# The low half of k in the score matmuls: a 64-row operand becomes a 128-row operand with 64 rows of zeros

## The chip, the cores and the metric

The kernel runs on one core of a Trainium2 chip. The metric is device time in microseconds (us) of that core, lower is better. TensorE is written PE (its weight loads PEld), VectorE DVE, ScalarE ACT, GpSimd POOL, and SP is the engine whose queue issues the DMAs.

## The reference, cut to what matters

One decoder layer over 272 rows (16 meta tokens and 256 positions), model width 2048, in float32. After a norm, one projection feeds eight attention heads and four retention heads; then an output projection, a gated MLP with a short convolution, and a last norm. The change concerns the scores of the attention heads. Each head h has two maps m = 0, 1 of depth 64:

```
aq, ak, av, rq, rk, rv, rg = jnp.split(proj, SPLITS, axis=-1)
...
s = jnp.einsum('bqhmd,bkhmd->bhmqk', qb, k).astype(jnp.float32) * scale
...
p = jax.nn.softmax(s, axis=-1)
a = (p[:, :, 0] - lam * p[:, :, 1]).astype(v.dtype)
return jnp.einsum('bhqk,bkhe->bqhe', a, v)
```

## The kernel before, in words

Float32 products are made from fp32r operands. A value x is split into hi (x rounded to fp32r) and lo (x - hi), and a product is the sum hi*hi + hi*lo + lo*hi.

**The projections (`gemm`, L243).** Activations lie with the model width over the 128 partitions, as `xhi` and `xlo`. Each block of 128 output columns takes 16 steps over the width, and each step three matmuls (L262 to L264) into one PSUM tile `mm`. The weights come by DMA as chunks of 1 MB (`raw`, three buffers, L87). ACT rounds each half chunk to `whi` (L99), DVE takes `wlo` as the difference (L100), three buffers each; `ahead` keeps two half chunks prepared beyond the one in use. After every quarter of a gemm, `pump` takes tasks from the list `side`: that is how attention work gets between the projection's matmuls. The framework's scheduler then fixes one order for each engine; the engines run their own order and meet by semaphores.

**The scores (L303).** A head's q and k stand in one tile of 128 partitions, map 0 in partitions 0 to 63 and map 1 in 64 to 127. From these the kernel makes, for each map m, a tile with all 128 partitions in use: `q2[:, m]` holds hi of q in the map's own 64 partitions (`hs`) and lo of q in the other 64 (`os`); `k2[:, m]` holds hi of k in both. So one matmul over 128 rows (L310) gives hi*hi + lo*hi. The third product, hi of q with lo of k, is a second matmul (L312) over the 64 partitions `hs` only, with lo of k in a tile `kl` of 128 x 272. A score task i (0, 1, 2) covers 86 queries and the first 100, 186 or 272 keys, and issues four matmuls: L310 and L312 for map 0, then L310 and L312 for map 1. The stationary operand, which PE loads first, is q (86 columns); k streams past it. There are 8 heads x 3 tasks = 24 score tasks, 96 matmuls, 48 of them at L312.

**The residual.** `htok` (128 x 2 x 2048 float32, 16 KB of each partition) is written only from the output projection on (L552) and lies unused before.

Of the kernel before, what the change touches and what calls it, by code (L numbers as in the profile page):

```python
# [10 lines left out]
F32 = mybir.dt.float32  # L11
F32R = mybir.dt.float32r
# [7 lines left out]
P = 128  # L20
D = 2048
# [3 lines left out]
T = META + SEQ  # L25
Q0 = META - 2
NQ = T - Q0
QT = NQ // 3
# [25 lines left out]
def trunk_kernel(ctx, tc, a, out):  # L54
# [84 lines left out]
    rstd1 = cp.tile([P, T], F32, name="rstd1")  # L139
    rstd2 = cp.tile([P, NQ], F32, name="rstd2")  # L140

    htok = big.tile([P, 2, D], F32, name="htok")
    ps1 = ctx.enter_context(tc.tile_pool(name="ps1", bufs=1, space=PSUM))

    def misc(name):
# [123 lines left out]
    with ExitStack() as p1:  # L269
# [5 lines left out]
        def row_rstd(ss, width, name):  # L275
# [7 lines left out]
            V.tensor_tensor(out=r, in0=r, in1=fin, op=ALU.mult)  # L283
            return r

        nop = lambda: None

        def att_tasks(h, q, k, v):
            slope = 2.0 ** (-(h + 1))
            tasks = []  # L290
            As = {}
            vt = ap_.tile([P, 3, P], F32, tag="vt", name=f"vt{h}")
            at = [ap_.tile([P, 3 - j, QT], F32, tag=f"at{j}", name=f"at{h}_{j}")
                  for j in range(3)]
            bias = ap_.tile([QT, 3, T], F32, tag="bias", bufs=1, name=f"bias{h}")

            def prelude():
                S.activation(out=bias, in_=base, func=AF.Copy, scale=slope)

            yo = ap_.tile([QT, 3, P], F32, tag="yo", name=f"yo_{h}")  # L300
            ss = sp.tile([QT, 3], F32, tag="ss3", name=f"ss{h}")

            def scores(i):  # L303
                def f():
                    nk = KB[i][1]
                    ps = ps1.tile([P, 2, 512], F32, tag="sc", bufs=1, name=f"sc{h}_{i}")
                    for m in range(2):
                        hs = slice(m * 64, (m + 1) * 64)
                        qs = slice(i * QT, (i + 1) * QT)
                        PE.matmul(ps[:QT, m, :nk], q[:, m, qs], k[0][:, m, :nk],  # L310
                                  start=True, stop=False)
                        PE.matmul(ps[:QT, m, :nk], q[hs, m, qs], k[1][hs, :nk],  # L312
                                  start=False, stop=True)
                    t = ap_.tile([QT, 2, T], F32, tag="t", name=f"t{h}_{i}")
                    nm = sp.tile([QT, 2], F32, tag="nm", name=f"nm{h}_{i}")
                    for m in range(2):
                        V.tensor_tensor_reduce(out=t[:, m, :nk], in0=bias[:, i, :nk],
                                               in1=ps[:QT, m, :nk], scale=-1.0, scalar=3.0e38,
                                               op0=ALU.add, op1=ALU.min,
                                               accum_out=nm[:, m:m + 1])  # L320
                    e = ap_.tile([QT, 2, T], F32, tag="e", name=f"e{h}_{i}")
                    sm = sp.tile([QT, 2], F32, tag="sm", name=f"sm{h}_{i}")
                    for m in range(2):
                        S.activation(out=e[:, m, :nk], in_=t[:, m, :nk], func=AF.Exp,
                                     bias=nm[:, m:m + 1], scale=-1.0,
                                     accum_out=sm[:, m:m + 1])
                    V.reciprocal(out=sm, in_=sm)
                    V.tensor_tensor(out=sm[:, 1:2], in0=sm[:, 1:2], in1=nlam[:QT], op=ALU.mult)
                    V.tensor_scalar(out=e[:, 0, :nk], in0=e[:, 0, :nk], scalar1=sm[:, 0:1],
                                    scalar2=None, op0=ALU.mult)  # L330
                    A = ap_.tile([QT, T], F32, tag="A", bufs=3, name=f"A{h}_{i}")
                    V.scalar_tensor_tensor(out=A[:, :nk], in0=e[:, 1, :nk], scalar=sm[:, 1:2],
                                           in1=e[:, 0, :nk], op0=ALU.mult, op1=ALU.add)
                    As[i] = A
                return f

            def vtr():
                ps = misc(f"pv{h}")
                for j, (b, e) in enumerate(KB):
                    PE.transpose(ps[:e - b, j * P:(j + 1) * P], v[:, b:e], idt)  # L340
                V.tensor_copy(out=vt[:KB[0][1], 0], in_=ps[:KB[0][1], :P])
                V.tensor_copy(out=vt[:QT, 1:3].rearrange("p a b -> p (a b)"),
                              in_=ps[:QT, P:3 * P])

            def atr(i):
                def f():
                    ps = misc(f"pa{h}_{i}")
                    for j in range(i + 1):
                        b, e = KB[j]
                        PE.transpose(ps[:e - b, j * P:j * P + QT], As[i][:, b:e], idt[:QT, :QT])  # L350
                    for j in range(i + 1):
                        b, e = KB[j]
                        (V.tensor_copy if j else S.copy)(
                            out=at[j][:e - b, i - j], in_=ps[:e - b, j * P:j * P + QT])
                return f

            def av():
                ps = misc(f"po{h}")
                for i in range(3):
                    for j in range(i + 1):  # L360
                        n = KB[j][1] - KB[j][0]
                        PE.matmul(ps[:QT, i * P:(i + 1) * P], at[j][:n, i - j], vt[:n, j],  # L362
                                  start=(j == 0), stop=(j == i))
                for i in range(3):
                    S.activation(out=yo[:, i], in_=ps[:QT, i * P:(i + 1) * P], func=AF.Square,
                                 accum_out=ss[:, i:i + 1])
                r = row_rstd(ss, P, f"ms{h}")
                for i in range(3):
                    S.activation(out=yo[:, i], in_=ps[:QT, i * P:(i + 1) * P], func=AF.Copy,
                                 scale=r[:, i:i + 1])  # L370

            def ytr():
                ps = misc(f"py{h}")
                for i in range(3):
                    PE.transpose(ps[:, i * QT:(i + 1) * QT], yo[:, i], idt[:QT, :QT])
                S.activation(out=yhi[:, h], in_=ps[:, :NQ], func=AF.Copy, scale=sub8)
                V.scalar_tensor_tensor(out=ylo[:, h], in0=ps[:, :NQ], scalar=sub8,
                                       in1=yhi[:, h].bitcast(F32), op0=ALU.mult,
                                       op1=ALU.subtract)

            return [prelude, scores(0), scores(1), vtr, scores(2), atr(0), atr(1), atr(2),
                    nop, av, nop, ytr]
# [94 lines left out]
        for h in range(AH):  # L477
            q = ap_.tile([P, NQ], F32, tag="q", name=f"q{h}")
            k = ap_.tile([P, T], F32, tag="k", name=f"k{h}")
            v = ap_.tile([P, T], F32, tag="v", name=f"v{h}")  # L480
            ps = gemm(idx, xhi, xlo, Q0, NQ, 1)
            V.scalar_tensor_tensor(out=q, in0=ps[:, :NQ], scalar=0.125, in1=rq_,
                                   op0=ALU.mult, op1=ALU.mult)
            ps = gemm(idx + 1, xhi, xlo, 0, T, 1)
            V.tensor_tensor(out=k, in0=ps[:, :T], in1=rk_, op=ALU.mult)
            ps = gemm(idx + 2, xhi, xlo, 0, T, 1)
            V.tensor_tensor(out=v, in0=ps[:, :T], in1=rk_, op=ALU.mult)
            idx += 3
            q2 = ap_.tile([P, 2, NQ], F32R, tag="q2", name=f"q2_{h}")
            k2 = ap_.tile([P, 2, T], F32R, tag="k2", name=f"k2_{h}")  # L490
            kl = ap_.tile([P, T], F32R, tag="kl", name=f"kl_{h}")
            for m in range(2):
                hs, os = slice(m * 64, m * 64 + 64), slice(64 - m * 64, 128 - m * 64)
                S.copy(out=q2[hs, m], in_=q[hs])
                V.tensor_tensor(out=q2[os, m], in0=q[hs], in1=q2[hs, m].bitcast(F32),
                                op=ALU.subtract)
                S.copy(out=k2[hs, m], in_=k[hs])
                V.tensor_copy(out=k2[os, m], in_=k[hs])
                V.tensor_tensor(out=kl[hs], in0=k[hs], in1=k2[hs, m].bitcast(F32),
                                op=ALU.subtract)  # L500
            side.extend(att_tasks(h, q2, (k2, kl), v))
        for kind, r in RSEQ:
# [16 lines left out]
            for c in range(2):  # L519
# [8 lines left out]
        ghi = Halves([big.tile([P, HK, NQ], F32R, tag=f"acthi{i}", name=f"ghi{i}")  # L528
                      for i in range(2)])
        glo = big.tile([P, KT, NQ], F32R, tag="actlo", name="glo")  # L530
        acc2 = yp.tile([P, NQ], F32, name="acc2")
        for j in range(KT):
            xr = ap_.tile([P, NQ], F32, tag="g0", name=f"xres{j}")
# [215 lines left out]
```

## Time and profile before

| | |
|---|---|
| time of three runs | 1216.55 to 1217.88 us, median 1217.49 us |
| span of the profiled execution | 1215.7 us (1.8 us less than the median) |
| PE busy, PEld busy | 98%, 93% of the span |
| DVE, ACT, POOL busy | 65%, 46%, 0% of the span |
| chain of work that ended last | PE 95%, DMA 2%, DVE 2% |

The profiled execution's own time is its span and the launch around it, which the span leaves out. The starts of matmuls and weight loads are recorded; the ends of matmuls are modelled, so what a matmul costs PE is read from its start to the start of the next one, called its pitch below. An engine's "busy" says little about whether it is at its peak.

### The profile page before, as it was taken

How to read it: one execution, taken by the hardware profiler on the slowest of the kernel's cores; microseconds unless marked ns; L12 is line 12 of the kernel's file. 1: busy time of each engine (PE TensorE's matmuls, PEld its weight loads, DVE VectorE, ACT ScalarE, POOL GpSimd, SP SyncE). 2: the span in 40 equal slices, each digit the busy share in tenths (PEclk: the TensorE clock that was granted, in tenths of full speed). 3: DMA queues.
4: the chain of work that ended last, by engine and by line, in shares of the span. 5: the costliest groups of instructions: out<-in, count | busy, mean ns of one | idle time of the engine just before them, and what ended most of it. 6: DMA issues, size and time to landing. Idle time of an engine off the chain costs nothing.

```text
span 1215.7 us, 21284 instructions
## 1 busy us (share of the span) xinstructions
PE 1196.5 (98%) x8811; PEld 1135.3 (93%) x8811; DVE 790.7 (65%) x1423; ACT 558.3 (46%) x865; POOL 0.8 (0%) x5
## 2 busy tenths in 40 slices
PE   7999999999999999999999999999999999999996
PEld 6999999999999999999999999999999988888885
DVE  6877787667786557666666666666666645454544
ACT  6465665544445554444444444444444434343442
POOL 0000000000000000000000000000000000000000
PEclk9999999999999999999999999999999999999998
DMA  8443343444445555554554554554555654555552
GB/s 295 149 168 108 140 142 138 163 165 146 153 164 200 196 191 175 193 188 174 189 193 174 184 198 174 179 197 180 177 195 184 210 202 177 196 185 187 194 180 98
DMA packets 34817, 215.71 MB, mean 177 GB/s; under 512 B 4194, under 2 KB 7882, under 8 KB 9760
## 3 DMA queue, kind: packets, MB, share of 16 engines
q1 hardware_dynamic: 34288, 212.58, 49.8%
q8 instruction: 69, 1.13, 0.4%
q0 software_dynamic: 144, 1.05, 0.3%
q10 hardware_dynamic: 288, 0.72, 0.2%
q14 instruction: 28, 0.23, 0.1%
HBM read 212.24 MB, written 2.10 MB: 176 GB/s over the span
## 4 chain that ended last, share of the span: by engine, by line
PE 95%; DMA 2%; DVE 2%; SPq 0%; ACT 0%; issue 0%; DVEq 0%; ACTq 0%
PE mm L262 23%; PE mm L263 23%; PE mm L264 23%; PE o L608 7%; PE o L609 7%; PE o L610 7%; DMA raw<-in_w_first_dram 1%; PE sc L312 1%; PE po L362 1%; PE sc L310 1%; DMA xr<-in_x_dram 1%; DVE wlo L100 0%; PE pa L350 0%; PE rs L402 0%; PE ph L551 0%
## 5 line engine op out<-in xcount | busy, mean ns | idle before, releaser
L99 ACT CAST whi<-raw 128x1024 fp32r<-128x1024 f32 x381 | 399.7, 1049 | 566.1 <-PE mm L263 309.0
L100 DVE TENSOR_TENSOR wlo<-raw,whi 128x1024 fp32r<-128x1024 f32 x381 | 466.3, 1224 | 280.9 <-ACT whi L99 278.0
L262 PE MATMUL mm<-ghi,whi 128*128 128x258 f32 (+1 forms) x1408 | 396.9, 282 | 0.0
L264 PE MATMUL mm<-ghi,wlo 128*128 128x258 f32 (+1 forms) x1408 | 396.7, 282 | 0.0
L263 PE MATMUL mm<-glo,whi 128*128 128x258 f32 (+1 forms) x1408 | 396.1, 281 | 0.0
L263 PEld LDWEIGHTS mm<-glo,whi 128*128 128x128 f32 x1408 | 266.4, 189 | 0.0
L262 PEld LDWEIGHTS mm<-ghi,whi 128*128 128x128 f32 x1408 | 266.0, 189 | 0.0
L264 PEld LDWEIGHTS mm<-ghi,wlo 128*128 128x128 f32 x1408 | 265.8, 189 | 0.0
L262 PE MATMUL mm<-xhi,whi 128*128 128x272 f32 (+1 forms) x688 | 201.5, 293 | 0.0
L263 PE MATMUL mm<-xlo,whi 128*128 128x272 f32 (+1 forms) x688 | 199.3, 290 | 0.0
L264 PE MATMUL mm<-xhi,wlo 128*128 128x272 f32 (+1 forms) x688 | 197.9, 288 | 0.6 <-DVE wlo L100 0.6
L609 PE MATMUL o<-wlo,fhi 128*128 128x512 f32 x340 | 134.1, 395 | 0.0
L610 PE MATMUL o<-whi,flo 128*128 128x512 f32 x340 | 134.1, 395 | 0.0
L262 PEld LDWEIGHTS mm<-xhi,whi 128*128 128x128 f32 x688 | 129.6, 188 | 1.5
L264 PEld LDWEIGHTS mm<-xhi,wlo 128*128 128x128 f32 x688 | 129.5, 188 | 1.0 <-DVE wlo L100 0.8
L263 PEld LDWEIGHTS mm<-xlo,whi 128*128 128x128 f32 x688 | 129.6, 188 | 0.7
L608 PE MATMUL o<-whi,fhi 128*128 128x512 f32 x340 | 120.8, 395 | 0.0
L609 PEld LDWEIGHTS o<-wlo,fhi 128*128 128x128 f32 x340 | 64.0, 188 | 15.0
L610 PEld LDWEIGHTS o<-whi,flo 128*128 128x128 f32 x340 | 64.1, 188 | 14.9
L608 PEld LDWEIGHTS o<-whi,fhi 128*128 128x128 f32 x340 | 64.0, 188 | 14.9
L262 PE MATMUL mm<-yhi,whi 128*128 128x258 f32 x256 | 73.3, 288 | 0.4 <-ACT whi L99 0.4
L263 PE MATMUL mm<-ylo,whi 128*128 128x258 f32 x256 | 72.4, 284 | 0.0
(226 smaller groups left out, 1071.4 us busy)
## 6 DMA issues: line engine op xcount, KB each, us to landing
raw<-in_w_in_dram SPq DMA_DIRECT2D x44, 1024.0 KB, 4.9
raw<-in_w_gate_dram SPq DMA_DIRECT2D x44, 1024.0 KB, 4.8
raw<-in_w_up_dram SPq DMA_DIRECT2D x44, 1024.0 KB, 4.8
raw<-in_w_down_dram SPq DMA_DIRECT2D x44, 1024.0 KB, 4.8
raw<-in_w_out_dram SPq DMA_DIRECT2D x16, 1024.0 KB, 4.9
xres<-in_x_dram SPq DMA_DIRECT2D x16, 129.0 KB, 3.8
raw<-in_w_first_dram SPq DMA_DIRECT2D x2, 1024.0 KB, 13.9
raw<-in_w_first_dram SPq DMA_DIRECT2D x3, 512.0 KB, 7.3
```

The lines of the kernel that those rows point to most:

```text
L99: S.copy(out=hi, in_=src)
L100: V.tensor_tensor(out=lo, in0=src, in1=hi.bitcast(F32), op=ALU.subtract)
L262: PE.matmul(ps[:, :n], wh, xh, start=(k == 0), stop=False)
L263: PE.matmul(ps[:, :n], wh, xl, start=False, stop=False)
L264: PE.matmul(ps[:, :n], wl, xh, start=False, stop=(k == KT - 1))
L310: PE.matmul(ps[:QT, m, :nk], q[:, m, qs], k[0][:, m, :nk], start=True, stop=False)
L312: PE.matmul(ps[:QT, m, :nk], q[hs, m, qs], k[1][hs, :nk], start=False, stop=True)
L362: PE.matmul(ps[:QT, i * P:(i + 1) * P], at[j][:n, i - j], vt[:n, j], start=(j == 0), stop=(j == i))
L608: PE.matmul(po[m], ah, wh, start=(k == 0), stop=False)
L609: PE.matmul(po[m], ah, wl, start=False, stop=False)
L610: PE.matmul(po[m], al, wh, start=False, stop=(k == NF - 1))
```

## The change

`kl` of each head moves out of the attention pool into a tile `klz` of 128 partitions x 2 slots (even and odd heads) x 2 maps x 272. `klz` takes the room of `htok`, which is now allocated after the attention and retention stage. Once, at the program's start, POOL sets to zero the 64 partitions of each map that hold no k (two instructions of 64 x 2 x 272). DVE writes lo of k into the map's own partitions as before, 64 x 272 for each map. The matmul at L312 (L315 afterwards) then takes all 128 partitions of `q2[:, m]` as stationary operand and all 128 of `klz` as the moving one: lo of q meets the zeros.

```
-    htok = big.tile([P, 2, D], F32, name="htok")
...
+        klz = big.tile([P, 2, 2, T], F32R, tag="htok", name="klz")
+        for m in range(2):
+            os = slice(64 - m * 64, 128 - m * 64)
+            nc.gpsimd.memset(klz[os, :, m].bitcast(F32), 0.0)
...
-                        hs = slice(m * 64, (m + 1) * 64)
                         qs = slice(i * QT, (i + 1) * QT)
                         PE.matmul(ps[:QT, m, :nk], q[:, m, qs], k[0][:, m, :nk],
                                   start=True, stop=False)
-                        PE.matmul(ps[:QT, m, :nk], q[hs, m, qs], k[1][hs, :nk],
+                        PE.matmul(ps[:QT, m, :nk], q[:, m, qs], k[1][:, m, :nk],
                                   start=False, stop=True)
...
-            kl = ap_.tile([P, T], F32R, tag="kl", name=f"kl_{h}")
+            kl = klz[:, h % 2]
...
-                V.tensor_tensor(out=kl[hs], in0=k[hs], in1=k2[hs, m].bitcast(F32),
+                V.tensor_tensor(out=kl[hs, m], in0=k[hs], in1=k2[hs, m].bitcast(F32),
                                 op=ALU.subtract)
...
+        htok = big.tile([P, 2, D], F32, tag="htok", name="htok")
```

The lines of the changed kernel are shifted: L262 to L264 become L261 to L263, L310 and L312 become L313 and L315. Apart from lines and buffer names, the rows of PE, DVE, ACT and SP stand in the same order as before, row for row. On POOL two rows are new. Before, at the program's start and end:

```order
L730 MEMSET const-float32-1.0 128x1
L730 MEMSET const-bfloat16-1.0 128x1
L730 MEMSET const-uint8-127 128x1
L738 UNCONDITIONAL_BRANCH [waits barrier_Pool_Activation_PE_DVE_SP_gather]
L592 DMA fn<-in_final_norm_dram 128x2048 [waits DVE_49,PE_49]
```

And in the changed kernel, with the memsets of `klz` ahead of the one DMA of that queue:

```order
L734 MEMSET const-float32-1.0 128x1
L734 MEMSET const-bfloat16-1.0 128x1
L734 MEMSET const-uint8-127 128x1
L742 UNCONDITIONAL_BRANCH [waits barrier_Pool_Activation_PE_DVE_SP_gather]
L288 MEMSET klz 64x2x272 x2
L596 DMA fn<-in_final_norm_dram 128x2048 [waits DVE_49,PE_49]
```

They wait for nothing of the kernel's own. On PE the first score task stands between two matmuls of the k projection. Before:

```order
L264 MATMUL mm_797<-xhi_68,wlo_736 128x272
L310 MATMUL sc_0_534<-k_0_462,q_0_461 86x100 [waits DVE_49]
L312 MATMUL sc_0_534<-kl_463,q_0_461 86x100
L310 MATMUL sc_0_534<-k_0_462,q_0_461 86x100
L312 MATMUL sc_0_534<-kl_463,q_0_461 86x100
L262 MATMUL mm_797<-xhi_68,whi_735 128x272
```

And in the changed kernel:

```order
L263 MATMUL mm_797<-xhi_68,wlo_736 128x272
L313 MATMUL sc_0_535<-k_0_464,q_0_463 86x100 [waits DVE_49]
L315 MATMUL sc_0_535<-klz,q_0_463 86x100 [waits Pool_49]
L313 MATMUL sc_0_535<-k_0_464,q_0_463 86x100
L315 MATMUL sc_0_535<-klz,q_0_463 86x100 [waits Pool_49]
L261 MATMUL mm_797<-xhi_68,whi_735 128x272
```

No row has moved; the two low matmuls of this first task now wait for the two memsets. Two more instructions gain that wait, both the first of their engine to write `htok`: ACT's first copy into it and DVE's first sum into it.

## Rows read from the trace of the kernel before

**Rows 1.** The page: the span, and the ending chain by engine.

```profile
span 1215.7 us, 21284 instructions
...
PE 95%; DMA 2%; DVE 2%; SPq 0%; ACT 0%; issue 0%; DVEq 0%; ACTq 0%
```

**Rows 2.** Busy time by stretch: engines, granted TensorE clock, DMA share, GB/s.

```profile
160.00:190.00 30.00, 30.00 (x232) 28.08 (x230) 24.31 (x84) 17.80 (x50) 0.00 (x0) 1.00 0.35 123
...
sum 154.00, PE 154.00 PEld 143.50 DVE 116.93 ACT 90.73 POOL 0.00; mean PE 30.80 PEld 28.70 DVE 23.39 ACT 18.15 POOL 0.00
```

**Rows 3.** Waits of PE between 58 and 290 us (total, times, longest).

```profile
PE mm L264 <- DVE wlo L100: 0.6, 1, 0.6
```

**Rows 4.** Tile `sc`: count, min/median/max ns, first and last start, forms.

```profile
L312 PE MATMUL sc<-kl,q x48: 275/314/354, 61.9 to 214.0; 64*86 64x100 f32 x16, 64*86 64x186 f32 x16, 64*86 64x272 f32 x16
```

**Rows 5.** Timeline of PE, first score task (start, length, engine, line).

```profile
61.73 0.21 PE L310 MATMUL sc<-k,q 128*86 128x100 f32 x1
...
62.08 0.28 PE L310 MATMUL sc<-k,q 128*86 128x100 f32 x1
62.29 0.28 PE L312 MATMUL sc<-kl,q 64*86 64x100 f32 x1
62.49 0.39 PE L262 MATMUL mm<-xhi,whi 128*128 128x272 f32 x1
62.73 0.28 PE L263 MATMUL mm<-xlo,whi 128*128 128x272 f32 x1
...
62.98 0.29 PE L262 MATMUL mm<-xhi,whi 128*128 128x272 f32 x1
```

**Rows 6.** Timeline of PE's weight loads in the same stretch.

```profile
61.61 0.15 PEld L310 LDWEIGHTS sc<-k,q 128*86 128x86 f32 x1
...
62.49 0.19 PEld L262 LDWEIGHTS mm<-xhi,whi 128*128 128x128 f32 x1
62.60 0.19 PEld L263 LDWEIGHTS mm<-xlo,whi 128*128 128x128 f32 x1
```

**Rows 7.** Timeline of PE, second score task of head 0.

```profile
66.63 0.25 PE L310 MATMUL sc<-k,q 128*86 128x186 f32 x1
...
67.78 0.29 PE L264 MATMUL mm<-xhi,wlo 128*128 128x272 f32 x1
```

**Rows 8.** Timeline of PE, third score task of head 0.

```profile
71.03 0.29 PE L310 MATMUL sc<-k,q 128*86 128x272 f32 x1
...
72.34 0.29 PE L263 MATMUL mm<-xlo,whi 128*128 128x272 f32 x1
```

**Rows 9.** Timeline of PE, L310 followed by matmuls over 86 rows.

```profile
133.07 0.21 PE L310 MATMUL sc<-k,q 128*86 128x100 f32 x1
133.12 0.39 PE L350 MATMUL pa<-c_ident,A 86*100 86x86 f32 x3
...
137.60 0.25 PE L310 MATMUL sc<-k,q 128*86 128x186 f32 x1
137.69 0.49 PE L362 MATMUL po<-vt,at 86*86 86x128 f32 x3
```

**Rows 10.** Weight loads by shape, 58 to 290 us (busy us, mean ns).

```profile
L262 PEld LDWEIGHTS mm<-xhi,whi 128*128 128x128 f32 x495 | 93.2, 188 | 1.4
L310 PEld LDWEIGHTS sc<-k,q 128*86 128x86 f32 x48 | 7.3, 153 | 2.3
```

**Rows 11.** Timeline of the program's start: memsets.

```profile
0.35 0.09 POOL L730 MEMSET const-uint8-127<- 128x1 uint8 x1
...
1.14 0.27 DVE L138 MEMSET warm<- 128x256 uint32 x1
```

**Rows 12.** Timeline of PE at the end of the first four projections.

```profile
30.05 0.58 PE L190 MATMUL mm<-xhi,whi 128*128 128x258 f32 x1 [3.88 <-ACT whi L182]
```

**Rows 13.** Timeline: one half chunk's `wlo` on DVE, its first matmul on PE.

```profile
76.34 1.22 DVE L100 TENSOR_TENSOR wlo<-raw,whi 128x1024 fp32r<-128x1024 f32 x1
...
80.02 0.29 PE L264 MATMUL mm<-xhi,wlo 128*128 128x272 f32 x1
```

## The prediction

> **What bounds the kernel now.** I read the page's chain first: PE holds 95% of what ended last, DMA and DVE 2% each [rows 1], so time taken from PE's sequence comes off the end unless another engine turns late. Next the stage in which the score tasks lie, 61 to 215 us: in the 154 us of the five stretches that cover it PE is busy for all 154.00, DVE for 116.93 (76%), ACT for 90.73 (59%), and the granted clock is 1.00, the 2.4 GHz level, in the stretch shown [rows 2]. Then PE's waits: between 58 and 290 us PE waited once, 0.6 us, for `wlo` [rows 3], and that is before the first score task. So PE is never held up by anything in this stage, and "busy" hides only what PE does badly by itself. That is read from starts alone.
>
> The first score task shows it. A projection matmul of 272 columns has a pitch of 0.125 us (62.73 to 62.98 is two of them). A score matmul streams only 100 columns, yet the 64-row one at 62.29 takes 0.20 us to the next start, and the projection matmul behind it takes 0.24 (62.49 to 62.73), double its usual pitch [rows 5]. The weight loads say why. For the L310 that follows a projection matmul, the load starts at 61.61, 0.12 us before its matmul starts at 61.73: loaded under the matmul ahead. The load for the projection matmul behind a 64-row matmul starts at 62.49, together with its matmul, and the next load is let go only at 62.60 [rows 5, 6]. On both sides of a 64-row matmul the load is not hidden; between 128-row matmuls it is. L310 itself has 86 columns of weights and short streams, so neither of these explains it. Nor does a row count below 128 as such: L310 of 100 columns followed by a matmul over 86 rows has a pitch of 0.05 us, and L310 of 186 columns one of 0.09 [rows 9]. What is special is 64.
>
> **The change part by part.** It removes the only 64-row matmuls, 48 of them, all between 61.9 and 214.0 us [rows 4]. I price one score task from the start of its first L310 to the start of the second projection matmul behind it, so that the doubled pitch is inside.
>
> Now: task 0 takes 62.73 - 61.73 = 1.00 us [rows 5], task 1 67.78 - 66.63 = 1.15 [rows 7], task 2 72.34 - 71.03 = 1.31 [rows 8]; together 3.46 us a head.
>
> After: five pitches each, with loads hidden. A pitch is the longer of its own stream and the next weight load. Loads: two loads of 128 columns follow each other after 0.11 us when nothing else holds them (62.49 to 62.60) [rows 6]; a load of 86 columns lasts 153 ns against 188 [rows 10], 35 ns less, so I take 0.074 us. Streams: 0.05 us for 100 columns, 0.09 for 186 [rows 9], 0.125 for 272 [rows 5].
> - Task 0: three pitches bound by an 86-column load, 3 x 0.074, one by the projection's 128-column load, 0.11, one projection matmul, 0.125: 0.457 us.
> - Task 1: 3 x 0.09 + 0.11 + 0.125 = 0.505 us.
> - Task 2: 5 x 0.125 = 0.625 us.
>
> Together 1.587 us a head, 1.87 less than now; eight heads give 15.0 us. Some tasks of later heads have transposes or value matmuls between the first L310 and its L312; these cost the same in both kernels, and the 64-row pitches around them are the same kind, so I price all heads like head 0.
>
> No row has two neighbouring 128-row loads of 86 columns, so 0.074 is an estimate from these rows. Its bounds: not below the stream of 0.05, not above the 128-column load of 0.11. With 0.05 task 0 gains 0.07 more, 0.6 us over eight heads. With 0.11 in tasks 0 and 1 the loss is 3 x 0.036 + 3 x 0.02 = 0.17 a head, 1.3 us. So PE gives back 13.7 to 15.6 us.
>
> That the matmuls stream 128 rows instead of 64 costs nothing extra: the 128-row L310 and the 64-row L312 of one task have the same pitch, 0.21 and 0.20 us from 62.08 on, where each stands beside the other [rows 5].
>
> Row against rule: the rows show that the load behind a 64-row matmul starts late, the load behind a 128-row one early [rows 5, 6]. The Trainium skill, "TensorE: Matmul & The Clock Gate", section on LDWEIGHTS, says that a weight load is priced by its columns, not by the rows it covers, 32 rows costing what 128 cost; its table of practical hints says the same of a single matmul of few rows. By that rule alone the edit would be worth 0, by the rows it is worth 15.0 us; the trace agrees with the rule on a single load (0.15 us for either row count) but not on when it may start.
>
> The zeros: two memsets of 64 x 544 on POOL, 1088 columns in all. The trace has no such POOL row. Bounds: DVE's memset of 256 columns took 0.27 us, 1.05 ns a column, so 1.1 us; POOL's memsets of one column took 0.09 us each [rows 11], which per column would be 98 us. I take the first, because 0.09 us for one column is what any small instruction costs, and price it at nothing: POOL has no other work, and the first reader is L312 at 61.9 us [rows 4], some 60 us later. Should the memsets hold up DVE or PE at the start, by a microsecond, PE's idle 3.88 us before 30.05 covers it [rows 12]; without that cover it would cost its own 1.1 us.
>
> At no cost either: DVE's writes into `klz` are the same 64 x 272, with the same waits; the slot of head h is written again for head h + 2, as with the two buffers before. The added waits on `htok` are for memsets long done. SP's rows are unmoved.
>
> **What is late next.** PE comes earlier by up to 15 us, so DVE and ACT must prepare weights faster: DVE's share of the stage rises from 76% to 116.93 / 139 = 84%, in the fullest stretch from 24.31 / 30 = 81% to about 90% [rows 2]. The preparation follows PE's releases, so it moves along; the smallest lead that I find inside the stage is the `wlo` that ends at 77.56 and is first read at 80.02, 2.46 us [rows 13]. By then four score tasks have given back 2.4 us, but DVE's own chain starts from those tasks' outputs and comes earlier too. I count no loss.
>
> Sum on the profiled execution: 1215.7 - 15.0 = 1200.7 us; the median of the runs stands 1.8 us above that span, so **1202.5 us**.
>
> **The rivals.**
> 1. The rows don't matter (the change doesn't do what it says): what holds the loads is the short 86-column operand. For: L310 has a pitch of 0.21 us inside the task too [rows 5]. Against: the projection matmul behind the task suffers too, and L310 behind a projection matmul does not. Time: 1217.5. Chance 5%.
> 2. DVE or ACT turn into the bound of the stage: half the gain is lost in waits for `wlo`. For: DVE near 90% and a lead of 2.46 us. Against: no wait in the stage now. Time: 1217.5 - 7.5 = 1210. Chance 5%.
> 3. Slower: POOL's memset is priced by the column at POOL's small rows. It would end near 0.4 + 98 us, L312 would wait from 61.9 to 98.4, 36.5 us, with every PE row behind it: 1202.5 + 36.5 = 1239. It costs from 61.5 us of memset on, and turns the sign at 61.5 + 15 + 2.4 = 79 us. For: only POOL's rows of one column are known. Against: four of those in a row were done 0.44 us into the span [rows 11]. Chance 4%.
>
> **How the numbers follow.** The forecast has 86%: 1202.5 us, with 13.7 to 15.6 us of gain and 0.7 us of spread between runs, that is 1201.2 to 1204.5. I widen it to 1200.8 to 1205.5 for a small loss in waits or a little more gain than the streams allow; this leaves out the rivals and about 5% of the forecast's own case. A difference of 0.2%, 2.4 us, is about what a measurement of this kernel can tell from no change. Faster: the forecast and rival 2, 91%. Same: rival 1, 5%. Slower: rival 3, 4%.
>
> **What would show it.** In the changed trace the loads of L315 and of the rows behind them start under the matmul ahead; pitches inside a task are near 0.075, 0.09 and 0.125 us, and no projection matmul behind a task takes 0.23. Head 0's three tasks, measured as above, sum to 1.6 us instead of 3.46. POOL shows two memsets of about a microsecond together, and PE no wait on POOL. Everything from 216 us on is the same work, 15 us earlier. The prediction is wrong if L315 still drags its load, if PE's waits in 61 to 200 us sum to more than a microsecond, or if the memsets reach 61 us.

## The result, and the profile after

The changed kernel takes 1201.6 us (median; 1200.84 to 1204.27) against 1217.4 us before: ratio 0.9878, 95% interval 0.9867 to 0.9890, which is 15.8 us less. 1202.5 us had been forecast.

The page of the changed kernel, its span, and the ending chain by engine and by line:

```profile
span 1199.9 us, 21288 instructions
...
PE 95%; DMA 2%; DVE 2%; SPq 0%; ACT 0%; issue 0%; DVEq 0%; ACTq 0%
PE mm L261 24%; PE mm L262 24%; PE mm L263 23%; PE o L612 7%; PE o L614 7%; PE o L613 7%; DMA raw<-in_w_first_dram 1%; PE po L365 1%; DMA xr<-in_x_dram 1%; PE sc L315 0%; PE sc L313 0%; DVE wlo L100 0%; PE pa L353 0%; PE rs L405 0%; SPq L165 0%
```

PE still holds 95% of the chain; in the full row, the two lines of the scores fell from 1% each to 0%. The first score task on PE's timeline, which answers to [rows 5]:

```profile
60.92 0.21 PE L313 MATMUL sc<-k,q 128*86 128x100 f32 x1
60.96 0.24 PE L315 MATMUL sc<-klz,q 128*86 128x100 f32 x1
61.04 0.24 PE L313 MATMUL sc<-k,q 128*86 128x100 f32 x1
61.12 0.24 PE L315 MATMUL sc<-klz,q 128*86 128x100 f32 x1
61.19 0.35 PE L261 MATMUL mm<-xhi,whi 128*128 128x272 f32 x1
61.38 0.29 PE L262 MATMUL mm<-xlo,whi 128*128 128x272 f32 x1
```

From the first start to the second projection matmul it takes 0.46 us instead of 1.00. The weight loads of the same stretch, which answer to [rows 6]:

```profile
60.80 0.15 PEld L313 LDWEIGHTS sc<-k,q 128*86 128x86 f32 x1
60.92 0.15 PEld L315 LDWEIGHTS sc<-klz,q 128*86 128x86 f32 x1
60.99 0.16 PEld L313 LDWEIGHTS sc<-k,q 128*86 128x86 f32 x1
61.07 0.16 PEld L315 LDWEIGHTS sc<-klz,q 128*86 128x86 f32 x1
61.15 0.19 PEld L261 LDWEIGHTS mm<-xhi,whi 128*128 128x128 f32 x1
61.26 0.19 PEld L262 LDWEIGHTS mm<-xlo,whi 128*128 128x128 f32 x1
```

Every load now starts 0.04 to 0.12 us before its matmul, also those of L315 and of the projection behind it; loads of 86 columns follow each other every 0.08 us. The other two tasks of head 0 on PE's timeline, from the first start to the second projection matmul behind as in [rows 7, 8], take 0.50 and 0.62 us instead of 1.15 and 1.31:

```profile
65.28 0.25 PE L313 MATMUL sc<-k,q 128*86 128x186 f32 x1
...
65.78 0.29 PE L263 MATMUL mm<-xhi,wlo 128*128 128x272 f32 x1
...
69.02 0.28 PE L313 MATMUL sc<-k,q 128*86 128x272 f32 x1
...
69.64 0.29 PE L262 MATMUL mm<-xlo,whi 128*128 128x272 f32 x1
```

The stage is now 139 us long. Its busy sums (PE, PEld, DVE, ACT, POOL) from the view by stretches, and PE's only wait between 40 and 275 us, which lies before the first score task (at 57 us) as it did in [rows 3]:

```profile
sum 139.00, PE 139.00 PEld 139.00 DVE 115.39 ACT 90.17 POOL 0.00; mean PE 27.80 PEld 27.80 DVE 23.08 ACT 18.03 POOL 0.00
```

```profile
PE mm L263 <- DVE wlo L100: 0.5, 1, 0.5
```

DVE's share is 115.39 / 139 = 83%. The lead that was smallest before [rows 13] is still the smallest of the stage; it has shrunk but holds; the `wlo` on DVE ends at 75.23 and is first read at 76.79, 1.56 us later:

```profile
74.00 1.23 DVE L100 TENSOR_TENSOR wlo<-raw,whi 128x1024 fp32r<-128x1024 f32 x1
...
76.79 0.29 PE L263 MATMUL mm<-xhi,wlo 128*128 128x272 f32 x1
```

**A measure that leaves out the start.** The way to the first score task differs by some microseconds between profiled executions (last section). So for each kernel I also give the time from the start of its first score matmul to the start of its last matmul, read from its one profiled execution. How far it can be trusted shows in kernels that should agree: the changed kernel, e4, e6 and e7 lie within 0.1 us of each other, the kernel before and e1 within 0.2 us.

| kernel | us, median | ratio, 95% interval | first score to last matmul, us | gain on it |
|---|---|---|---|---|
| before | 1217.4 | | 1143.8 | |
| after | 1201.6 | 0.9867 to 0.9890 | 1128.8 | 15.0 |
| e1, layout alone | 1217.2 | 0.9984 to 1.0003 | 1143.7 | 0.1 |
| e2, map 1 alone | 1208.5 | 0.9912 to 0.9941 | 1136.1 | 7.7 |
| e3, 64 rows, side by side | 1207.5 | 0.9905 to 0.9935 | 1134.4 | 9.4 |
| e4, map 0 over 96 rows | 1200.7 | 0.9847 to 0.9876 | 1128.9 | 14.9 |
| e5, without low product | 1199.4 | 0.9842 to 0.9871 | 1125.5 | 18.3 |
| e6, long memsets | 1202.4 | 0.9868 to 0.9897 | 1128.8 | 15.0 |
| e7, 128 rows in e3's order | 1201.9 | 0.9860 to 0.9893 | 1128.9 | 14.9 |
| e8, 64 rows, cut in two | 1209.4 | 0.9918 to 0.9955 | 1136.3 | 7.5 |

### The profile page after: what moved, and what is told of

It is laid out like the page before. It is cut to its first block, busy times and chain, and to the rows that moved or that the text cites. A ratio compares the mean times of both kernels' runs of the same rounds, so it can differ in the third digit from the quotient of the medians.

```text
span 1199.9 us, 21288 instructions
## 1 busy us (share of the span) xinstructions
PE 1183.2 (99%) x8811; PEld 1132.3 (94%) x8811; DVE 790.1 (66%) x1423; ACT 557.5 (46%) x865; POOL 2.0 (0%) x7
## 4 chain that ended last, share of the span: by engine, by line
PE 95%; DMA 2%; DVE 2%; SPq 0%; ACT 0%; issue 0%; DVEq 0%; ACTq 0%
PE mm L261 24%; PE mm L262 24%; PE mm L263 23%; PE o L612 7%; PE o L614 7%; PE o L613 7%; DMA raw<-in_w_first_dram 1%; PE po L365 1%; DMA xr<-in_x_dram 1%; PE sc L315 0%; PE sc L313 0%; DVE wlo L100 0%; PE pa L353 0%; PE rs L405 0%; SPq L165 0%
## 5 line engine op out<-in xcount | busy, mean ns | idle before, releaser
L261 PE MATMUL mm<-ghi,whi 128*128 128x258 f32 (+1 forms) x1408 | 396.9, 282 | 0.0
L263 PE MATMUL mm<-ghi,wlo 128*128 128x258 f32 (+1 forms) x1408 | 396.7, 282 | 0.0
L262 PE MATMUL mm<-glo,whi 128*128 128x258 f32 (+1 forms) x1408 | 396.1, 281 | 0.0
L262 PEld LDWEIGHTS mm<-glo,whi 128*128 128x128 f32 x1408 | 266.4, 189 | 0.0
L261 PEld LDWEIGHTS mm<-ghi,whi 128*128 128x128 f32 x1408 | 266.0, 189 | 0.0
L263 PEld LDWEIGHTS mm<-ghi,wlo 128*128 128x128 f32 x1408 | 265.8, 189 | 0.0
L261 PE MATMUL mm<-xhi,whi 128*128 128x272 f32 (+1 forms) x688 | 200.4, 291 | 0.0
L262 PE MATMUL mm<-xlo,whi 128*128 128x272 f32 (+1 forms) x688 | 198.8, 289 | 0.0
L263 PE MATMUL mm<-xhi,wlo 128*128 128x272 f32 (+1 forms) x688 | 197.8, 288 | 0.5 <-DVE wlo L100 0.5
L263 PEld LDWEIGHTS mm<-xhi,wlo 128*128 128x128 f32 x688 | 129.5, 188 | 0.8 <-DVE wlo L100 0.8
L261 PEld LDWEIGHTS mm<-xhi,whi 128*128 128x128 f32 x688 | 129.7, 188 | 0.1
L262 PEld LDWEIGHTS mm<-xlo,whi 128*128 128x128 f32 x688 | 129.6, 188 | 0.1
L613 PEld LDWEIGHTS o<-wlo,fhi 128*128 128x128 f32 x340 | 64.1, 188 | 14.9
L612 PEld LDWEIGHTS o<-whi,fhi 128*128 128x128 f32 x340 | 64.0, 188 | 14.9
L261 PE MATMUL mm<-yhi,whi 128*128 128x258 f32 x256 | 73.2, 288 | 0.4 <-ACT whi L99 0.4
L262 PE MATMUL mm<-ylo,whi 128*128 128x258 f32 x256 | 72.3, 283 | 0.0
```

The costliest lines, as they stand in the source:

```text
L261: PE.matmul(ps[:, :n], wh, xh, start=(k == 0), stop=False)
L262: PE.matmul(ps[:, :n], wh, xl, start=False, stop=False)
L263: PE.matmul(ps[:, :n], wl, xh, start=False, stop=(k == KT - 1))
L612: PE.matmul(po[m], ah, wh, start=(k == 0), stop=False)
L613: PE.matmul(po[m], ah, wl, start=False, stop=False)
```

## The experiments

**e1: the layout without the matmul.** Edit to the changed kernel:

```
+                        hs = slice(m * 64, (m + 1) * 64)
...
-                        PE.matmul(ps[:QT, m, :nk], q[:, m, qs], k[1][:, m, :nk],
+                        PE.matmul(ps[:QT, m, :nk], q[hs, m, qs], k[1][hs, m, :nk],
```

> The changed kernel with everything but its matmul: klz in the room of htok, the two memsets and the later htok stay, the low matmuls take 64 rows again. Theory (the whole gain comes from PE no longer changing between 128-row and 64-row matmuls): the time of before, 1217.4 us, with the three score tasks of head 0 at 1.00, 1.15 and 1.31 us. Rival (part of the gain comes from the new places in SBUF or from the later htok): between 1202 and 1216 us. If the 0.8 us that the changed kernel was ahead before its first score task came from the memsets, this run is ahead by them too, 1216.6.

1217.2 us: no gain. The three tasks of head 0 take 0.99, 1.15 and 1.30 us, as before. The rival of the layout falls. The 0.8 us by which the changed kernel's profile was ahead at its first score task (60.92 against 61.73) did not come back with the memsets: e1 has them and started its scores at 62.48. One start can't exclude a part of the memsets in it, because the starts differ by more than that (last section), and the interval of this run's time is too wide to tell 0.8 us.

**e2: only map 1 over 128 rows.** With `hs = slice(0, 64 + m * 64)` in the same matmul, map 0 keeps 64 rows.

> The changed kernel with only map 1's low matmul over 128 rows, map 0's over 64. Theory: every 64-row matmul exposes the load into it and the loads behind it, whatever else stands in the task. Worked out from pitches of before and after, the tasks take 0.73, 0.82 and 0.95 us (2.50 a head, against 3.46 and 1.59), so 7.6 us of the 15 come: 1209.8 us. Rival (one 64-row matmul spoils the whole task): under 3 us of gain, 1215 or more. Rival (what costs is map 1's matmul, whose operands start at partition 64): nearly the whole gain, 1203 or less.

1208.5 us, 7.7 us on the measure without the start, where 7.6 had been worked out, and tasks of 0.73, 0.82 and 0.95 us as expected: a 64-row matmul that stands between 128-row ones pays for itself, whatever the other map does. Both rivals fall, the one of 1215 us or more and the one of 1203 or less. PE's timeline of the first task shows both kinds:

```profile
60.08 0.21 PE L314 MATMUL sc<-k,q 128*86 128x100 f32 x1
60.22 0.28 PE L316 MATMUL sc<-klz,q 64*86 64x100 f32 x1
60.42 0.28 PE L314 MATMUL sc<-k,q 128*86 128x100 f32 x1
60.54 0.24 PE L316 MATMUL sc<-klz,q 128*86 128x100 f32 x1
60.62 0.35 PE L261 MATMUL mm<-xhi,whi 128*128 128x272 f32 x1
60.81 0.29 PE L262 MATMUL mm<-xlo,whi 128*128 128x272 f32 x1
```

Pitches of 0.14, 0.20 and 0.12 us around the 64-row matmul (into it, out of it, and the one behind), 0.08 from the 128-row low matmul to the projection.

**e3: 64 rows, both low matmuls next to each other.** Edit to the kernel before:

```
+                    qs = slice(i * QT, (i + 1) * QT)
+                    for m in range(2):
+                        PE.matmul(ps[:QT, m, :nk], q[:, m, qs], k[0][:, m, :nk],
+                                  start=True, stop=False)
                     for m in range(2):
                         hs = slice(m * 64, (m + 1) * 64)
-                        qs = slice(i * QT, (i + 1) * QT)
-                        PE.matmul(ps[:QT, m, :nk], q[:, m, qs], k[0][:, m, :nk],
-                                  start=True, stop=False)
                         PE.matmul(ps[:QT, m, :nk], q[hs, m, qs], k[1][hs, :nk],
                                   start=False, stop=True)
```

> The kernel before with one edit: in each score task both L310 first, then both 64-row low matmuls, so that PE changes once into 64 rows and once out of it. Theory (the change between row counts costs, not the 64-row matmul): the second 64-row matmul's load is hidden, tasks near 0.70, 0.84 and 0.98 us, gain 7.5 us: 1209.9 us. Rival (each 64-row matmul pays for itself): only the pitch between the two L310 shrinks, gain 3.6 us: 1213.8 us. Variant of the theory (two 64-row matmuls on different rows run side by side): a pitch near 0 between the two, gain up to 9 us, 1208.5 us. The scheduler places some other rows differently here.

1207.5 us, and tasks of 0.66, 0.76 and 0.86 us, shorter than the theory's 0.70, 0.84 and 0.98: the rival of 1213.8 falls, and the variant fits best. PE's timeline of the first task ("x2" is two matmuls in a row):

```profile
60.75 0.29 PE L309 MATMUL sc<-k,q 128*86 128x100 f32 x2
60.97 0.28 PE L313 MATMUL sc<-kl,q 64*86 64x100 f32 x2
61.18 0.39 PE L262 MATMUL mm<-xhi,whi 128*128 128x272 f32 x1
61.41 0.29 PE L263 MATMUL mm<-xlo,whi 128*128 128x272 f32 x1
```

From the first 64-row start to the projection's are 0.21 us, as from a single one in the kernel before (0.20 in [rows 5]): the second one is free, and only the change into 64 rows and the change out of it are paid, 0.66 us for this task against 0.46 in the changed kernel. The task of 272 keys shows the same with longer streams: two 64-row matmuls take 0.28 us together in e3 (69.69 to 69.97), and a single one took 0.28 in the kernel before (71.82 to 72.10), so the two streams don't follow each other. The Trainium skill, "TensorE: Matmul & The Clock Gate", Part 3 on packing small matmuls, says that matmuls on different row groups run at the same time; the trace agrees.

**e4: map 0 over 96 rows, map 1 over 128.** With `hs = slice(0, 96 + m * 32)`.

> The changed kernel with map 0's low matmul over 96 rows (64 of k, 32 of zeros), map 1's over 128. Theory (only the 64-row case makes PE change its way of working): the same as the changed kernel, 1201.6 us, all pitches the same. Rival (any operand below 128 rows drags its loads): half of the gain is lost, 1209.8 us as with map 0 over 64 rows.

1200.7 us, and 14.9 us on the measure without the start: 96 rows are as good as 128. A row count below 128 doesn't drag as such: 64 does, 96 doesn't, and other counts were not tried in this place.

**e5: no low matmul.** The second `PE.matmul` of the score task is left out, the first one stops the sum.

> The changed kernel without the low matmuls: hi of q with lo of k is left out of the scores, so this prices what the 48 zero-padded matmuls still cost. Theory (they cost their pitches of the changed kernel's trace and nothing else): two pitches of 0.076, 0.087 and 0.124 us less in the three tasks, 0.574 us a head, 4.6 us in all: 1197.0 us against 1201.6. Rival (PE is by now ahead of DVE and ACT, so that shorter tasks turn into waits): 1199 us or more, with waits of PE for wlo or for a score tile. The scheduler places other rows differently here.

1199.4 us, 3.3 us less than the changed kernel on the measure without the start, where 4.6 were expected. Summed by tile, the pitches of the score matmuls fell by 4.7 us (9.33 to 4.67), close to the 4.6 worked out; 1.4 us came back elsewhere, in rows that the scheduler had placed differently: the projections' matmuls cost 0.9 us more, of which about 0.8 in one gap at a wait for DVE, the retention's matmuls 0.9 more, and the other small matmuls 0.5 less. The time lies in the rival's range, but the wait is not one that the rival named: PE waited for `rg`, the DVE product that empties a PSUM tile of a projection, and not for `wlo` or a score tile. From the view of PE's waits:

```profile
PE mm L261 <- DVE rg L508: 0.6, 1, 0.6
```

So the zero-padded matmuls cost 4.7 us of PE's pitches; the 64-row ones, with what they did to their neighbours, cost 15.0 us more.

**e6: long memsets.** Three more memsets over the rest of the room of `htok`, 128 x 3008 each:

```
+        for c in range(3):
+            nc.gpsimd.memset(room[:, 4 * T:].bitcast(F32), 0.0)
```

> The changed kernel with POOL also setting the rest of htok's room to zero, three memsets of 128 x 3008, before the two of klz; at 0.57 us for 544 columns that is 3.2 us each, 10.6 us in all. It prices the memsets and the cover at the start. Theory (a POOL memset holds up DVE's cast of onesr until it ends, as in the changed kernel where that cast took 0.63 us instead of 0.16; the delay is covered by PE's waits for data at the start): DVE's cast takes 3 us or more, PE's first projection matmuls come up to some us later, the time stays within 1 us of the changed kernel's 1201.6. Rival (the delay stays on the path): 1204 us or more. Rival (POOL and DVE don't meet at all): the cast takes 0.16 us.

1202.4 us, and no difference on the measure without the start. The timelines of POOL and DVE (the scheduler put one long memset ahead of the two short ones):

```profile
0.74 2.60 POOL L288 MEMSET room<- 128x3008 f32 x1 [0.29 <-POOLq L737]
3.40 1.15 POOL L291 MEMSET room<- 64x544 f32 x2
...
1.33 2.09 DVE L136 CAST onesr<-one 128x128 fp32r<-128x128 f32 x1
3.54 0.50 DVE L174 SCALAR_TENSOR_TENSOR xlo<-xr,xhi 128x272 fp32r<-128x272 f32 x1
```

The cast is held until just after the long memset ends at 3.34. It was 2.09 us and not the expected 3 or more, since only one of the long memsets ran ahead of it; the rival of 0.16 falls. The next DVE instruction is not held by the memsets that still run: it takes 0.50 us, as in the kernel before. The cover named in the prediction was hardly needed, since DVE's first instruction on input data started at 3.54 here and at 3.44 in the kernel before, where no memset ran. Whether a held cast would cost anything without it was not tried.

**e7: 128 rows in e3's order.** e3's loops in the changed kernel.

> The changed kernel with the order of the run that put both 64-row matmuls side by side: both high matmuls first, then both low ones, all over 128 rows. Theory (only the row count matters, the order of 128-row matmuls doesn't): the same as the changed kernel, 1201.6 us, the pitch between the two low matmuls 0.08 to 0.125 us, not 0.003. Rival (the order alone gave part of that run's 9.9 us): faster than 1200 us.

1201.9 us, and 1128.9 on the measure without the start against 1128.8: the order is worth nothing by itself; what e3 gained, it gained by 64-row matmuls meeting.

**e8: 64-row matmuls behind each other on the same rows.** Edit to e3:

```
-                        PE.matmul(ps[:QT, m, :nk], q[hs, m, qs], k[1][hs, :nk],
-                                  start=False, stop=True)
+                        for c in (slice(0, nk // 4 * 2), slice(nk // 4 * 2, nk)):
+                            PE.matmul(ps[:QT, m, c], q[hs, m, qs], k[1][hs, c],
+                                      start=False, stop=c.stop == nk)
```

> The run with both 64-row matmuls side by side, with each of them cut into two over half of the keys: map 0 twice, then map 1 twice, so that a 64-row matmul follows another on the same rows. It asks whether the cost lies in the change between 128 and 64 rows or in 64-row weights, which might never be loaded ahead over rows that are in use. Theory (the change): the pitch between the two halves of one map is a hidden load, about 0.075 us, and 24 tasks x 0.11 us more make 2.6 us on top of that run's 1207.5: 1210.1 us. Rival (64-row weights on the same rows are never loaded ahead): that pitch is the unhidden one of before, 0.19 to 0.22 us, and the time 8.9 us more than that run's: 1216.4 us.

1209.4 us, near the theory and far from the rival's 1216.4. PE's timeline of the first task:

```profile
61.45 0.29 PE L309 MATMUL sc<-k,q 128*86 128x100 f32 x2
61.67 0.34 PE L314 MATMUL sc<-kl,q 64*86 64x50 f32 x4
61.94 0.40 PE L262 MATMUL mm<-xhi,whi 128*128 128x272 f32 x1
```

Four 64-row matmuls take 0.27 us together where e3's two took 0.21, and a single one 0.20 before: among themselves they hide their loads. So it is the change between 64 and 128 rows that costs. The starts within the four don't follow the expected even pitch (the two halves of one map are recorded 7 ns apart, the maps 91 ns), so the recorded starts inside such a group aren't read as times of work, in e3 neither; the sums over the group are.

No version beat the changed kernel without leaving work out; e4 is the same within its interval.

## Why the prediction was right

**The mechanism.** What it read from starts alone was confirmed from three sides: the gain comes with the matmul and not with the layout (e1), half of it with one of the two maps (e2), and not from the row count as such (e4). e3 and e8 sharpen the wording: what PE pays for is the change between 128 and 64 rows, once in and once out, not each 64-row matmul. The Trainium skill, "TensorEngine Tiling (Array Packing)", Key Properties, says that changing the tiling mode drains TensorE while changing the tile does not; these runs agree. The rule weighed in the prediction, that rows don't matter to a load, holds for one load and says nothing of when it may start; rival 1 is excluded by e1 against the changed kernel.

**The sum.** Forecast 15.0 us for 24 tasks; measured 15.0 us on the measure without the start, 1143.8 to 1128.8. The 24 tasks, each measured as in the prediction, fell from 30.99 to 16.15 us together, 14.8 of it. By tile, the pitches of the score matmuls fell by 12.1 us, those of the projections' by 1.9, and those of the transposes and value matmuls near them by 1.0. The prediction held that these last cost the same in both kernels; what it needed is that a task with them gains as much as one without, and that came: the longest fell from 2.03 to 1.39 us, 0.64, where 0.65 had been priced for such a task. Tasks of head 0: 0.46, 0.50 and 0.62 us where 0.457, 0.505 and 0.625 were worked out. The estimate of 0.074 us for an 86-column load measured 0.08. Inside task 0 two pitches were placed wrongly: the first L313 to L315 is 0.04 and not 0.074, and the last low matmul to the projection 0.07 and not 0.11, while the projection matmul then takes 0.19 and not 0.125. The starts of the loads, shown in the section on the result, have the sum as it was worked out: 0.07, 0.08, 0.08 and 0.11 us from the load at 60.92 to the one at 61.26, and 0.12 from there to its matmul at 61.38. The matmuls within this chain start 0.04 or 0.05 us after their loads, those at its two ends 0.12. So the sum was right, but its place among the matmuls' pitches was not.

**What was costed at nothing.** The memsets took 1.14 us for 1088 columns, the lower bound taken (1.1); rival 3 would have cost time from 61.5 us on and turned the sign at 79. PE has no wait on POOL. They did hold DVE's cast at the start, 0.63 us against 0.16, which had only been allowed for as a possibility. The cast in the kernel before, from DVE's timeline:

```profile
1.33 0.16 DVE L136 CAST onesr<-one 128x128 fp32r<-128x128 f32 x1
```

From the timelines of POOL and DVE in the changed kernel:

```profile
0.75 1.14 POOL L288 MEMSET klz<- 64x544 f32 x2 [0.29 <-POOLq L734]
...
1.35 0.63 DVE L136 CAST onesr<-one 128x128 fp32r<-128x128 f32 x1
```

**Rival 2** did not come: DVE's share rose to 83% (84% worked out), its smallest lead fell to 1.56 us, PE waited for nothing in the stage. How much of this lead could still be used is not shown: in e5, with another order, the smallest lead of a `wlo` was 1.40 us without a wait for one, and PE's one wait in the stage was for DVE's `rg`.

**The rest.** The medians differ by 15.8 us, 0.8 more than the sum. The profiles show 0.8 us of it before the first score task, in a stretch that the change touches only by the cast. There PE went on after its wait for weights at 30.05 us before and at 29.77 after, and from 30 to 36 us the granted clock was 0.58 before and 0.72 after, with 30 and 37 matmuls started; the 24 us behind that have 188 in both. So I put it down to the spread of the start: e1 has the same memsets and started later than either. That no part of it comes from the change is argued from these profiles and not shown apart; the medians of the kernel before, measured four times, differ by as much (1216.7 to 1217.4).

## What to carry to other kernels

Here short matmuls over 64 rows between matmuls over 128 cost their neighbours more than themselves: of the 15.0 us that padding gave back, 6.8 lay in their own pitches and 8.2 in those of others. Look at the starts of weight loads, not at durations, and pad such an operand with zeros to 96 or 128 rows, where there is room for the zeros. If it can't be padded, put 64-row matmuls on different halves of the rows next to each other, so that the change is paid once for several (9.4 of the 15.0 us here). Where PE was full and never waited, a sum of start-to-start pitches foretold the gain to a fraction of a microsecond (15.0 and 15.0 for the change, 7.6 and 7.7 in e2); in e5, where other rows moved and a wait came in, it was 1.3 us off.

## What had not been expected of the hardware

- A POOL memset held back a DVE cast from SBUF to SBUF until it ended (0.16 us became 0.63, and 2.09 with a memset of 2.60 us), but not DVE's scalar_tensor_tensor, which ran at 3.54 us beside the next memset in e6 in its usual 0.50 us. The Trainium skill, "SBUF — State Buffer", Who interferes with whom, says that GpSimd and DVE's two-port instructions, which casts can be, lock each other out for a whole instruction, while an instruction with two SBUF inputs isn't held by a GpSimd write; the trace agrees.
- The start spreads. The first score task began between 59.25 (e4) and 62.48 us (e1), with the same work ahead of it. Around 30 us PE waits for the last weights of the first projections, 4.31 us in e1 and 2.29 in e4; in the 6 us from 30 us on the granted clock was 0.50, the 1.2 GHz level, in e1 and 1.00, the 2.4 GHz level, in e4. In the other eight profiles, with waits of 2.88 to 4.75 us, it lay between 0.58 and 0.81, and not in the order of the waits. The rows by stretch (PEclk is the third number from the end), e1 first, then e4:

```profile
30.00:36.00 6.00, 5.66 (x25) 5.66 (x26) 4.48 (x5) 2.45 (x4) 0.00 (x0) 0.50 0.34 97
```

```profile
30.00:36.00 6.00, 5.99 (x47) 5.70 (x46) 5.25 (x7) 2.53 (x3) 0.00 (x0) 1.00 0.45 158
```

In the same 6 us PE started 25 matmuls in the one and 47 in the other. So a difference of a microsecond between two of these kernels is better read behind this stretch than from the whole time.
